# A sliding-window copy: one megabyte moves to the software ring, in parts that are uneven over the DMA engines

## The chip, the cores and the metric

The kernel runs on one core of one Trainium2 chip. The metric is the device time of one execution in microseconds (us). Medians are of three to eleven runs. Two kernels are compared only within one call, on one chip. Four chips come up: "the first" (the prediction and its result), and "the second", "the third" and "the fourth". Where a stretch of one trace is set beside that of another chip, the text says so.

## The reference

```python
def reference(x, window_size, stride):          # x: 32 x 4096 x 256 float32, 64, 32
    batch, length, dim = x.shape
    n_windows = (length - window_size) // stride + 1            # 127
    result = np.zeros((batch, n_windows, window_size, dim), dtype=np.float32)
    for i in range(n_windows):
        start = i * stride
        result[:, i] = x[:, start:start + window_size].copy()
    return result
```

No arithmetic: of HBM, the large memory beside the chip's cores, 134 MB are read and 266 MB written. A window is 64 KB, two consecutive blocks of 32 rows (32 KB each), and each inner block is written twice.

## The kernel before

Three queues feed the same 16 DMA engines. The ACT queue loads every third batch into on-chip memory (11 batches) and stores it twice. The Sync queue copies most of the other batches from HBM to HBM directly, sixteen windows at a time. The software ring, issued by GpSimd, copies what doesn't fit the sixteens ("edges" of fifteen windows, then the last few windows), once the Sync queue is almost done.

```python
    def windows(self, q, b, w0, n, half=None, piece=DIRECT):      # DIRECT = 32768 bytes
        blk = self.blk
        row = [1, 2 * blk if half is None else blk]
        h = half or 0
        return q.dma_start(
            out=self.oap((b * self.nw + w0) * 2 + h, [[2 * blk, n], row]),
            in_=self.xap(b * self.nb + w0 + h, [[blk, n], row]),
            max_dma_last_dim=piece,
        )
# ... columns(): the same with rows cut in 16 parts of 4 KB; load() and store(): the ACT queue's ...

    first_loads, loads, stores = 6 * 17, 5 * 17, 6 * 34
    turns = share = 0
    with tc.tile_critical():
        st.run(ring_s)                                            # all of the ACT queue's work
        for i, (b, w) in enumerate(sixteens):
            sem = near if i == len(sixteens) - 2 else done
            second = turns - first_loads - stores
            loading = turns < first_loads or 0 <= second < loads
            share += 120 if turns < 16 or -8 <= second < 16 else 90 if loading else 18
            if share >= 120:
                share -= 120
                turns += 4
                count(c.windows(ring_d, b, w, 16, 0), done)       # two copies of half rows
                count(c.windows(ring_d, b, w, 16, 1), sem)
            else:
                turns += 3
                count(c.windows(ring_d, b, w, 16), sem)           # one copy of whole rows
            # ... one window by itself, half way ...
        ring_r.wait_ge(near, 16)
        for b, w, n in edges:
            # ... waits for stores of the neighbouring batches ...
            count(c.windows(ring_r, b, w, n), rest)
        count(c.columns(ring_r, last, 116, 9), rest)
        # ... Sync's last two windows, then waits for everything ...
```

`turns` counts packets: an engine serves its queues by turns, one packet each. A whole-row copy gives an engine two packets of 32 KB and a semaphore packet (three turns for 64 KB), a split one two of each (four turns). The share of split ones therefore sets how much the ACT queue moves meanwhile, and so whether all queues end together.

Of the kernel before, what the change touches and what calls it, by code (L numbers as in the profile page):

```python
# [11 lines left out]
class Copier:  # L12
# [27 lines left out]
    def columns(self, q, b, w0, n):  # L40

        part = self.blk // 8
        row = [1, part]
        return q.dma_start(  # L44
            out=self.oap((b * self.nw + w0) * 2, [[part, 16], [2 * self.blk, n], row]),
            in_=self.xap(b * self.nb + w0, [[part, 16], [self.blk, n], row]),
        )

    def load(self, q, t, b, c, rows):
# [76 lines left out]
@with_exitstack  # L126
def kernel(
    ctx: ExitStack,
    tc: tile.TileContext,
    x: bass.AP,  # L130
    window_size: bass.AP,
    stride: bass.AP,
    out: bass.AP,
):
    nc = tc.nc
    W, S = int(window_size), int(stride)
    B, L, D = x.shape
    n_win = (L - W) // S + 1
    assert out.shape == (B, n_win, W, D)
    c = Copier(x, out, B, L, D, W, S, n_win)  # L140


    staged = [*range(1, B, 3)]
    items = [(b, -1 if b == B - 1 else 0, c.nb) for b in staged]
    place = {b: g for g, (b, _, n) in enumerate(items) if n == c.nb}
    direct = [b for b in range(B) if b not in staged]
    pool = ctx.enter_context(tc.tile_pool(name="xb", bufs=1))
    st = Staging(c, tc, pool, x.dtype, items, 6)
    ring_d, ring_s, ring_r = nc.sync, nc.scalar, nc.gpsimd
    done = tc.alloc_semaphore("done")  # L150
    near = tc.alloc_semaphore("near")
    rest = tc.alloc_semaphore("rest")
    total = {done: 0, near: 0, rest: 0}

    def count(dma, sem):
        dma.then_inc(sem, 16)
        total[sem] += 16



    sixteens = []
    for b in direct:
        w = 15 if b - 1 in staged else 0
        sixteens += [(b, w + 16 * j) for j in range((c.nw - w) // 16)]
    singles = [(B - 1, c.nw - 1, 1)]
    edges = [(b, 0 if b - 1 in staged else 112, 15) for b in direct[:-1]]
    last = B - 2
    edges.append((last, 112, 4))

    first_loads, loads, stores = 6 * 17, 5 * 17, 6 * 34  # L170
    turns = share = 0
    with tc.tile_critical():  # L172
        st.run(ring_s)

        for i, (b, w) in enumerate(sixteens):
            sem = near if i == len(sixteens) - 2 else done
            second = turns - first_loads - stores
            loading = turns < first_loads or 0 <= second < loads
            share += 120 if turns < 16 or -8 <= second < 16 else 90 if loading else 18
            if share >= 120:  # L180
                share -= 120
                turns += 4
                count(c.windows(ring_d, b, w, 16, 0), done)
# [3 lines that stand above are left out]
                count(c.windows(ring_d, b, w, 16), sem)  # L187
            if i == len(sixteens) // 2:
                for b, w, half in singles:
                    count(c.windows(ring_d, b, w, 1, half, 2048), done)  # L190

        ring_r.wait_ge(near, 16)
        for b, w, n in edges:
            for k in (b - 1, b + 1):
                if k in place and b != last:
                    st.wait_stored(ring_r, place[k])
            count(c.windows(ring_r, b, w, n), rest)


        count(c.columns(ring_r, last, 116, 9), rest)  # L200
        st.wait_stored(ring_d, place[B - 1])
        count(c.columns(ring_d, last, 125, 2), done)
        total[st.ended] = st.count[st.ended]
        for sem, n in total.items():
            ring_d.wait_ge(sem, n)
# [35 lines left out]
```

## Time and profile before

| kernel before, first chip | |
|---|---|
| median (3 runs) | 752.05 us |
| bytes moved by the DMA engines, mean rate | 313.26 MB, 418 GB/s |
| Sync's last 32 KB packet ends | 656.7 us |
| first ring packet | 658.7 us |
| last data packet of ACT; of the ring | 745.1 us; 745.8 us |

The first lines are from the page of the profile of the kernel before. The rows of 40 give, in slices of 18.7 us, the tenths for which the 16 DMA engines were busy and the GB/s moved. Then come the number of packets, and for each queue its packets, megabytes and share of the engines' time (q1 is Sync, q10 ACT, q0 the ring).

```profile
DMA  8999999999999999999999999999999999999996
GB/s 360 401 427 429 427 429 428 434 423 418 420 424 423 418 424 415 422 427 427 414 427 417 429 432 429 430 422 430 429 423 421 423 421 419 425 426 423 431 409 262
DMA packets 18290, 313.26 MB, mean 418 GB/s; under 512 B 4336, under 2 KB 4336, under 8 KB 4528
...
q1 hardware_dynamic: 8016, 154.32, 48.8%
q10 hardware_dynamic: 9104, 138.41, 44.0%
q0 software_dynamic: 1168, 20.51, 6.5%
...
HBM read 220.95 MB, written 267.09 MB: 651 GB/s over the span
```

The engines are at least nine tenths busy in every slice between the first and the last, so only three things can be gained: a faster start, a faster rate, a shorter end. In the trace's packet records an undisturbed packet of 32 KB takes 1.213 us and one of 16 KB 0.611 us, which is 27 GB/s for an engine and some 432 GB/s for sixteen.

The same view restricted to two stretches: the 15 us from the ring's first packet, and twelve microseconds shortly before the end.

```profile
DMA packets 351, 6.54 MB, mean 436 GB/s; under 512 B 73, under 2 KB 73, under 8 KB 73
...
q0 software_dynamic: 181, 3.97, 62.6%
q10 hardware_dynamic: 170, 2.57, 40.6%
```

Last, the ring's groups of instructions (line, engine, operation, count, then busy us and mean ns, then the idle time before them and what ended it): 22 copies, the first issued when Sync signalled at 654 us.

```profile
L34 POOL DMA_DIRECT2D out_dram<-in_x_dram x21 | 12.0, 576 | 691.3 <-DMA out_dram<-in_x_dram 654.0
L44 POOL DMA_DIRECT2D out_dram<-in_x_dram x1 | 0.6, 581 | 0.0
```

### The profile page before, as it was taken

What the parts mean: (1) busy time and instruction counts of PE and PEld (TensorE: products, weight loads), DVE (VectorE), ACT (ScalarE), POOL (GpSimd) and SP (SyncE); (2) the same over time, 40 slices, a digit from 0 to 9 for tenths busy, and PEclk for the clock granted to TensorE, in tenths of its full rate; (3) what the DMA queues carried; (4) which work ended last, traced back from release to release, by engine and by line L of the source; (5) the groups of instructions that cost most, each with busy time, mean ns of one, the idle gap of its engine ahead of it and who ended that gap; (6) DMA issues with size and microseconds to landing.
All of it is one profiled execution on the core that took longest, in us unless ns stands there. A gap on an engine that the chain in (4) does not pass through costs nothing.

```text
span 749.4 us, 322 instructions
## 1 busy us (share of the span) xinstructions
POOL 12.8 (2%) x26
## 2 busy tenths in 40 slices
POOL 0000000000000000000000000000000000040100
DMA  8999999999999999999999999999999999999996
GB/s 360 401 427 429 427 429 428 434 423 418 420 424 423 418 424 415 422 427 427 414 427 417 429 432 429 430 422 430 429 423 421 423 421 419 425 426 423 431 409 262
DMA packets 18290, 313.26 MB, mean 418 GB/s; under 512 B 4336, under 2 KB 4336, under 8 KB 4528
## 3 DMA queue, kind: packets, MB, share of 16 engines
q1 hardware_dynamic: 8016, 154.32, 48.8%
q10 hardware_dynamic: 9104, 138.41, 44.0%
q0 software_dynamic: 1168, 20.51, 6.5%
q14 instruction: 2, 0.02, 0.0%
HBM read 220.95 MB, written 267.09 MB: 651 GB/s over the span
## 4 chain that ended last, share of the span: by engine, by line
another core or an unknown queue 92%; POOL 2%; issue 0%; POOLq 0%; SPq 0%
POOL out_dram L34 2%; POOL out_dram L44 0%; POOLq L236 0%; SPq L172 0%; POOLq L114 0%
## 5 line engine op out<-in xcount | busy, mean ns | idle before, releaser
L34 POOL DMA_DIRECT2D out_dram<-in_x_dram x21 | 12.0, 576 | 691.3 <-DMA out_dram<-in_x_dram 654.0
L44 POOL DMA_DIRECT2D out_dram<-in_x_dram x1 | 0.6, 581 | 0.0
L222 POOL MEMSET const-float32-0.0<- 128x1 f32 x1 | 0.1, 98 | 0.2 <-issue 0.2
L222 POOL MEMSET const-bfloat16-1.0<- 128x1 bf16 x1 | 0.1, 101 | 0.0
L222 POOL MEMSET const-float32-1.0<- 128x1 f32 x1 | 0.1, 98 | 0.0
L222 POOL MEMSET const-uint8-127<- 128x1 uint8 x1 | 0.1, 98 | 0.0
## 6 DMA issues: line engine op xcount, KB each, us to landing
out_dram<-in_x_dram SPq DMA_DIRECT2D x92, 1024.0 KB, 100.7
out_dram<-xb ACTq DMA_DIRECT2D x21, 4096.0 KB, 139.7
out_dram<-in_x_dram SPq DMA_DIRECT2D x110, 512.0 KB, 90.3
xb<-in_x_dram ACTq DMA_DIRECT2D x10, 4096.0 KB, 131.4
out_dram<-in_x_dram POOLq DMA_DIRECT2D x20, 960.0 KB, 38.5
xb<-in_x_dram ACTq DMA_DIRECT2D x4, 1024.0 KB, 15.7
out_dram<-xb ACTq DMA_DIRECT2D x2, 1024.0 KB, 113.4
out_dram<-xb ACTq DMA_DIRECT2D x4, 512.0 KB, 96.9
```

The source lines that it names most:

```text
L34: return q.dma_start(out=self.oap((b * self.nw + w0) * 2 + h, [[2 * blk, n], row]), in_=self.xap(b * self.nb + w0 + h, [[blk, n], row]), m ...
L44: return q.dma_start(out=self.oap((b * self.nw + w0) * 2, [[part, 16], [2 * self.blk, n], row]), in_=self.xap(b * self.nb + w0, [[part, 16 ...
L222: nc = _bacc.Bacc("TRN2", target_bir_lowering=False, num_devices=1)
```

## The change

The last sixteen windows of the Sync queue (1 MB) go to the ring. In a cycle of the head every engine makes one 32 KB copy and two 16 KB loads. The intent is to set groups of four engines apart by a quarter of that cycle: at the outset three copies of four rows each give 48, 32 and 16 KB to an engine of three groups; the fourth group gets nothing. The remainder follows when Sync is almost done, so that each engine has carried 64 KB. The three constants of the split pattern are retuned for it.

```diff
+    def quarters(self, q, b, w0, p0, n):
+        part = self.blk // 4
+        at = p0 * 2 * part
+        dims = [[part, 2 * n], [1, part]]
+        return q.dma_start(
+            out=bass.AP(self.out.tensor, self.oap((b * self.nw + w0) * 2, dims).offset + at, [[2 * self.blk, 4], *dims]),
+            in_=bass.AP(self.x.tensor, self.xap(b * self.nb + w0, dims).offset + at, [[self.blk, 4], *dims]),
+            max_dma_last_dim=4 * part,
+        )
@@
+    apart = sixteens.pop()
@@
     with tc.tile_critical():
+        for k in range(3):
+            count(c.quarters(ring_r, apart[0], apart[1] + 4 * k, 0, 3 - k), rest)
         st.run(ring_s)
@@
-            share += 120 if turns < 16 or -8 <= second < 16 else 90 if loading else 18
+            share += 120 if turns < 28 or -8 <= second < 16 else 86 if loading else 11
@@
         ring_r.wait_ge(near, 16)
+        for k, p in ((3, 0), (0, 3), (1, 2), (2, 1)):
+            count(c.quarters(ring_r, apart[0], apart[1] + 4 * k, p, 4 - p), rest)
```

`max_dma_last_dim` is in bytes, so 4 * part is 8 KB: the parts go as packets of 8 KB, 6, 4 and 2 to an engine at the outset, 8, 2, 4 and 6 at the end.

## The prediction

> **What bounds it now.** The kernel only moves bytes: the page's DMA part shows 313.26 MB at a mean of 418 GB/s over 749.4 us, the 16 DMA engines busy 9 tenths or more in slices 2 to 39; the chain of waits is 92% DMA. In the trace's packet records an undisturbed 32 KB packet takes 1.213 us, a 16 KB one 0.611, so 16 engines reach about 432 GB/s; 313.26 MB at that rate is 725 us. The missing 24 us:
> - first packet at 2.4 us;
> - a slow head: 239, 393, 405 GB/s up to 8 us, 430 up to 16, then 368 to 404 up to 32 us (16 KB load packets take up to 2.0 us), then 432;
> - 410 to 425 GB/s in most store stretches (32 KB packets at 1.24 to 1.26 us), some 12 us in sum;
> - a drain: engines finish between 740.8 and 745.8 us, the span ends 3.6 us later.
>
> Up to 16 us all engines are in step: a 32 KB direct copy, then two 16 KB loads, a cycle of 2.43 us. From 50 us on phases are scattered.
>
> **What the change does.** 1 MB leaves the Sync queue for the software ring. At the outset three copies with four outer rows give 48, 32, 16 and 0 KB to four groups of engines; the remainder (16, 32, 48, 64 KB) follows when the Sync queue is almost done. The Trainium skill, "DMA: Bandwidth & Descriptors", section "Why a DMA increments its semaphore by 16 and not by 1", says that a software-ring copy with k below 16 runs on k consecutive engines from a round-robin cursor; four rows then mean four engines. No view of before shows it. 16 KB is 0.61 us, a quarter cycle: the groups should run a quarter cycle apart, so copies (HBM read and write) and loads (read only) mix evenly at once, not after 34 us. Split pairs on the Sync queue fall from 55 to 48, with the moved block 10 turns per engine fewer; Sync ends some us before its present 656.7 us and leaves ACT about 2.5 MB more for the last stretch. The ring's small packets give turns back to ACT, so I expect ring and ACT still to end together.
>
> **Costs.** No byte added. 8 packets of 8 KB instead of 2 of 32 KB per engine, at some 10 ns fixed each (2 x 0.611 - 1.213), and seven semaphore packets of 9 ns: 0.1 us. Ring packets came 4.3 us after issue at 654 us; at the outset I expect them at 3 to 5 us. The issues (0.58 us each) are on an idle engine.
>
> **On the critical path.** Only the head and, by chance, the drain. Lost against 432 GB/s: 17 us at about 390 (1.6 us), 0.6 us at 4 to 8 us, 0.4 us at 43 to 48: 2.6 us. I expect over half back, 1.5 to 2 us. The store stretches have scattered phases already: nothing changes there. The drain may move by 1 to 2 us either way.
>
> **Prediction: 750.2 us, range 747.6 to 752.6; faster by over 2%: 0.01, within 2%: 0.98, slower by over 2%: 0.01.**
>
> **Right shows as:** 0.38 MB of 8 KB ring packets before 8 us on 12 engines; slices 1 and 2 above 365 and 415 GB/s; 16 to 32 us above 415; middle slices as before; drain again 5 us wide. **Wrong:** the dip persists though groups are staggered (then addresses, not phases); ring packets come too late; ring or ACT ends well ahead; the lag of 48 KB widens the drain.
>
> **What would make it wrong.** Uneven engine speeds decide the drain; the copies may not land on distinct groups; slow store stretches may depend on the queues' shares, which the new split pattern moves.

## More of the kernel before

```profile
DMA packets 375, 4.94 MB, mean 411 GB/s; under 512 B 135, under 2 KB 135, under 8 KB 172
...
q0 software_dynamic: 165, 2.94, 59.8%
q10 hardware_dynamic: 162, 1.87, 38.2%
q1 hardware_dynamic: 48, 0.13, 2.8%
```

The view counts a packet where it starts, so a short stretch can show a little more than 432 GB/s. As soon as the ring starts, it takes 3.97 MB of 6.54 and ACT 2.57; near the end both still run side by side. That mix matters: the ring's copies read and write HBM, ACT's stores only write it.

## The result, and the profile after

The changed kernel is slower: 756.08 us (755.71 to 756.55, 6 runs) against 751.9 us, ratio 1.0055, 95% interval 1.0041 to 1.0068. A ratio is the mean time of one kernel's fast runs over that of the other's of the same rounds, so it is not quite the ratio of the quoted medians. The time lies above the range predicted.

The same lines of the page of the changed kernel:

```profile
DMA  8999999999999999999999999999999999999996
GB/s 360 419 428 429 425 425 429 429 419 421 418 422 417 425 412 425 421 425 423 409 424 412 433 419 423 431 430 428 423 418 425 412 424 416 426 415 433 412 398 220
DMA packets 18754, 313.26 MB, mean 415 GB/s; under 512 B 4704, under 2 KB 4704, under 8 KB 4896
...
q1 hardware_dynamic: 7856, 153.27, 48.3%
q10 hardware_dynamic: 9104, 138.41, 43.8%
q0 software_dynamic: 1792, 21.56, 7.2%
...
HBM read 220.95 MB, written 267.09 MB: 647 GB/s over the span
```

The bytes are the same. The ring has 624 packets more, and only 128 of them are the megabyte in packets of 8 KB. The other 496 are packets of 4 bytes. The packet records show what they are. While a four-row copy runs, each of the four engines that carry it has a packet of 8 KB where each of the twelve others has one of 4 bytes; then all sixteen have one more, the semaphore's. That makes 12 x 32 + 16 x 7 = 496, without remainder. The kernel before follows the same rule: its 20 edges of two packets leave one engine idle, the copy of four windows leaves twelve, the one in columns none, and 20 x (2 + 16) + (12 x 2 + 16) + 16 = 416.

So the seven copies occupy 32 + 7 turns on every engine, data or not: 15 at the outset, 24 at the end. The kept records do not name the engine of a packet; what runs on which is read from these counts and from the times. The 15 us from the ring's first packet at the end show the price:

```profile
DMA packets 748, 6.43 MB, mean 429 GB/s; under 512 B 320, under 2 KB 320, under 8 KB 320
...
q10 hardware_dynamic: 374, 5.65, 88.9%
q0 software_dynamic: 374, 0.78, 13.4%
```

Ring and ACT have 374 packets each, one for one. But by the packet records the ring's are 291 of 4 bytes, 79 of 8 KB and 4 of 32 KB, and ACT's are 345 of 16 KB and 29 of 4 bytes (the semaphores'), so ACT moves 5.65 MB and the ring 0.78, where before the ring moved 3.97. Sync ended at 651.6 us, the ring's first packet came at 653.4 us, its first large copy at 667.8 us. By then ACT had 11.7 MB left; before, it had 14.7 MB at the same point. ACT then runs out first, as ten microseconds near the end show:

```profile
DMA packets 207, 3.51 MB, mean 351 GB/s; under 512 B 82, under 2 KB 82, under 8 KB 90
...
q0 software_dynamic: 165, 3.15, 89.5%
q10 hardware_dynamic: 42, 0.36, 10.1%
```

The engines are as busy as ever, yet move 351 GB/s. The ring's 32 KB packets take some 1.48 us here instead of 1.21. The ring's bytes are both read from and written to HBM, ACT's only written; with each packet shared out over its duration, these ten microseconds carry 671 GB/s of HBM traffic. The Trainium skill, "HBM Reference", section "Specifications (TRN2)", gives about 716 GB/s for a domain, and this stretch lies somewhat below that. So a limit of HBM fits, but it is argued and not shown: the first stretch of the kernel before carried as much, 670 GB/s by the same count, while half of the ring's 32 KB packets took the undisturbed 1.213 us. What is shown is that the rate falls when the ring is left alone; with ACT's stores beside it, 12 us near the end ran at 411 GB/s before.

The ring's groups of instructions after the change:

```profile
L54 POOL DMA_DIRECT2D out_dram<-in_x_dram x7 | 4.3, 624 | 646.7 <-DMA out_dram<-in_x_dram 645.6
L34 POOL DMA_DIRECT2D out_dram<-in_x_dram x21 | 11.9, 571 | 29.9 <-DMA out_dram<-xb 29.9
L44 POOL DMA_DIRECT2D out_dram<-in_x_dram x1 | 0.6, 573 | 0.0
```

There are 29 copies instead of 22. The trace's records of the last instructions, which these views leave out, show a second price. After all data has landed, a drain on GpSimd takes 2.437 us, where it took 1.865 us before. From the last data packet to the end of the span it is 4.6 us, 3.6 us before.

### The profile page after: what moved, and what is told of

Read it like the earlier page. It is cut to its first block, busy times and chain, and to the rows that moved or that the text cites. A ratio compares the mean times of both kernels' runs of the same rounds, so it can differ in the third digit from the quotient of the medians.

```text
span 754.8 us, 320 instructions
## 1 busy us (share of the span) xinstructions
POOL 17.0 (2%) x33
## 4 chain that ended last, share of the span: by engine, by line
another core or an unknown queue 89%; POOL 2%; issue 0%; PEldq 0%
POOL out_dram L34 2%; POOL out_dram L54 1%; POOL out_dram L44 0%; PEldq L254 0%
## 5 line engine op out<-in xcount | busy, mean ns | idle before, releaser
L54 POOL DMA_DIRECT2D out_dram<-in_x_dram x7 | 4.3, 624 | 646.7 <-DMA out_dram<-in_x_dram 645.6
L34 POOL DMA_DIRECT2D out_dram<-in_x_dram x21 | 11.9, 571 | 29.9 <-DMA out_dram<-xb 29.9
L44 POOL DMA_DIRECT2D out_dram<-in_x_dram x1 | 0.6, 573 | 0.0
```

What stands on the lines that cost most here:

```text
L34: return q.dma_start(out=self.oap((b * self.nw + w0) * 2 + h, [[2 * blk, n], row]), in_=self.xap(b * self.nb + w0 + h, [[blk, n], row]), m ...
L44: return q.dma_start(out=self.oap((b * self.nw + w0) * 2, [[part, 16], [2 * self.blk, n], row]), in_=self.xap(b * self.nb + w0, [[part, 16 ...
L54: return q.dma_start(out=bass.AP(self.out.tensor, self.oap((b * self.nw + w0) * 2, dims).offset + at, [[2 * self.blk, 4], *dims]), in_=bas ...
```

## The experiments

Theory A: the ring's empty turns hold its large copies back at the end, ACT drains alone, then the ring copies alone at some 350 GB/s. Rival B: the new split pattern costs. Rival C: the lag itself, or the moved megabyte, widens the drain of the engines. Theory D, for the last microsecond: the closing drain grows with the number of ring copies. Expectations in microseconds were written for the first chip (before: 751.9 us) and are read as ratios.

| run | chip | median, us | before, us | ratio | 95% interval |
|---|---|---|---|---|---|
| changed kernel | first | 756.08 | 751.9 | 1.0055 | 1.0041 to 1.0068 |
| split pattern alone (e1_shares_only) | second | 746.68 | 745.51 | 1.0010 | 0.9998 to 1.0022 |
| parts, old split pattern (e2_parts_old_shares) | second | 751.01 | 745.51 | 1.0075 | 1.0063 to 1.0088 |
| parts as whole rows (e3_whole_rows) | second | 748.70 | 745.51 | 1.0040 | 1.0028 to 1.0052 |
| remainder after the edges (e4_rest_late) | second | 747.39 | 745.51 | 1.0024 | 1.0013 to 1.0036 |
| before, again (b0_before_again) | third | 745.48 | 745.45 | 1.0000 | 0.9989 to 1.0012 |
| changed, again (a0_after_again) | third | 749.06 | 745.45 | 1.0050 | 1.0038 to 1.0063 |
| before, nine ring copies for one (e5_nine_columns) | third | 746.62 | 745.45 | 1.0013 | 1.0001 to 1.0025 |
| parts on all 16 engines (e6_even_parts) | third | 746.36 | 745.45 | 1.0010 | 0.9996 to 1.0024 |
| two packets to a row (e7_two_packets) | fourth | 746.13 | 745.01 | 1.0020 | 1.0006 to 1.0034 |
| remainder in 4 KB packets (e9_half_packets_late) | fourth | 754.07 | 745.01 | 1.0119 | 1.0106 to 1.0133 |

### The split pattern alone

```diff
 kernel before
-            share += 120 if turns < 16 or -8 <= second < 16 else 90 if loading else 18
+            share += 120 if turns < 28 or -8 <= second < 16 else 86 if loading else 11
```

> The kernel before with the three new constants of the split pattern alone (28, 86, 11), no parts. Theory A (the four-row copies put a 4-byte packet on the 12 idle engines for each of their packets, so the remainder at the end holds the ring's large copies back for 24 turns, ACT drains alone, and the ring then copies alone at some 350 GB/s): about 751.5 us, within 750 to 753, since ACT then outlasts the ring a little and costs nothing. Rival B (the new split pattern costs: slower middle, other balance): 754 to 756 us, and bytes moved by 650 us about 0.8 MB behind before.

The ratio is 1.0010, within theory A's range (751.5 of 751.9 is 0.9995, 753 is 1.0015) and below rival B's. Bytes moved by 640 us are 272.13 MB; the kernel before, on the third chip, where it takes as long, moved 272.28. B falls: the pattern is not what costs.

### The parts with the old split pattern

```diff
 changed kernel
-            share += 120 if turns < 28 or -8 <= second < 16 else 86 if loading else 11
+            share += 120 if turns < 16 or -8 <= second < 16 else 90 if loading else 18
```

> The changed kernel with the old constants (16, 90, 18). Theory A: still held back by 24 turns, and ACT has about 1.6 MB less left when the Sync queue ends (16.3 instead of 17.9 MB), so the ring is alone for longer: 756 to 758 us, slower than the changed kernel. Rival B: 750 to 752 us.

The ratio is 1.0075, worse than the changed kernel, as theory A said. At the first large ring copy ACT has 10.1 MB left; ACT ends at 731.3 us, the ring at 744.1. The retuned constants were right in direction: they leave ACT more for the end. They do not make up for 24 turns.

### The parts as whole rows

```diff
 changed kernel
-        dims = [[part, 2 * n], [1, part]]
+        dims = [[1, 2 * n * part]]
-            max_dma_last_dim=4 * part,
+            max_dma_last_dim=DIRECT,
```

> The changed kernel with the same bytes as whole rows of 16 to 32 KB, so 10 turns of packets instead of 32 (6 instead of 20 at the end). Theory A: the 4-byte packets of the software ring fall from 912 to 648 (12 x 10 + 7 x 16 + 416), the first 32 KB ring packet of the large copies comes about 6 us after the ring's first packet at the end instead of 15, ring and ACT end together, 749.5 to 751.5 us. Rival B: 754 to 756 us still.

This run missed. The 4-byte packets are 648, as counted, and ACT and ring end within a microsecond of each other (740.3 and 741.3 us). But the ratio is 1.0040, in rival B's range. One microsecond is the longer end, found here first (4.6 us after the last packet). Another difference is seen in the packets of the head. By their times, a copy of 32 KB rows and one of 16 KB rows, one packet to an engine, landed on the same four engines as the first copy, so these four were given 96 KB and the others nothing; the ring did not move on. The edit changed two things, then, and does not test theory A cleanly. The last edit but one below does.

### The remainder after the edges

```diff
 changed kernel
-        for k, p in ((3, 0), (0, 3), (1, 2), (2, 1)):
-            count(c.quarters(ring_r, apart[0], apart[1] + 4 * k, p, 4 - p), rest)
         for b, w, n in edges:
             ...
+        for k, p in ((3, 0), (0, 3), (1, 2), (2, 1)):
+            count(c.quarters(ring_r, apart[0], apart[1] + 4 * k, p, 4 - p), rest)
         count(c.columns(ring_r, last, 116, 9), rest)
```

> The changed kernel with the remainder issued after the ring's large copies instead of before them, its form unchanged. Theory A: the large copies start some 2 us after the Sync queue ends, ACT and ring run together to the end, 750 to 752 us although every packet and filler is there. Rival B, and rival C (the lag of 48 KB itself or the moved megabyte widens the drain): 754 us or more.

All packets and all empty turns are still there (912 of 4 bytes), only later. The ring's large copies start at 646.5 us, 1.4 us after Sync ends; ACT and ring end at 738.4 and 740.2 us. The ratio falls to 1.0024, half of the changed kernel's. That is under the range of B and C (754 is 1.0028, which the interval still includes), and above that of A (752 is 1.0001), which did not know of the longer end: 4.5 us after the last packet here too.

### Both kernels once more, on one chip

No edit.

> The kernel before, unchanged, for its profile and noise beside the others of this call. All theories: ratio 1.000 within 0.002; ring's last clean-up on GpSimd about 1.87 us. If the head's dip of the first profile (12.6 MB by 34 us, 19.4 MB by 50 us) is a steady trait of this kernel, it is there again; if it was chance, up to 0.7 MB more by 50 us.

> The changed kernel, unchanged, beside the others. Theory A: ratio about 1.005 to 1.006 on this chip as well, first large ring copy about 15 us after the ring's first packet at the end, ACT done some 5 us or more before the ring, and 340 to 360 GB/s in the stretch that the ring copies alone; bytes moved by 650 us within 0.3 MB of before's (the 0.8 MB deficit of the first pair of profiles was chance).

The ratios are 1.000 and 1.005. The two spans are 743.6 and 747.7 us, and the packet records divide the 4.1 us between them:

- Up to 640 us the changed kernel moved 272.05 MB, the one before 272.28: 0.5 us. The profiles of the second and third chip lie between 271.9 and 272.4 MB (without the one that fell on its kernel's slowest run), so this is not told from chance.
- From 640 us to the last packet, 41.0 MB took 100.0 us before and 41.2 MB took 103.2 us after: 2.6 us beyond the 0.5.
- From the last packet to the end: 3.6 us before, 4.6 us after: 1.0 us.

The middle term has two parts, found by asking when each kernel had moved the same number of bytes. From 285 to 305 MB the two go at the same pace. The last 8 MB cost 1.5 us, and these are theory A's: the first large ring copy comes at 661.8 us, 14.8 us after the ring's first packet; ACT ends at 736.4 us, the ring at 743.2; from 728 to 740 us the rate is some 355 GB/s.

The other 1.0 us is lost between 280 and 285 MB, just where the ring's large copies begin and ACT still has plenty. Theory A has no place for it. The packet records of all runs give the rate in the ten microseconds from the first large ring copy on:

| before that copy, the ring had | GB/s in the ten microseconds |
|---|---|
| nothing at the end: kernel before (first, third chip), e1, e5, e4 | 429, 428, 431, 431, 430 |
| the remainder on all 16 engines: e6 | 422 |
| the remainder on groups of four: changed kernel (first, third chip), e2, e3, e7, e9 | 397, 390, 403, 393, 400, 379 |

For e3 and e7, whose remainder has 32 KB packets too, the start of the large copies is counted off from the number of those. So the uneven remainder has a second price, 0.6 to 1.2 us if 430 GB/s is taken as the undisturbed rate (an estimate from this table). It is a comparison of traces that were made for other questions; why the rate dips was not tested.

In the first chip's pair of profiles the changed kernel was also 0.8 MB, 1.9 us, behind by 640 us. The third chip's pair, 0.2 MB apart, does not repeat it.

The head answers the prediction's main point. From 16 to 34 us the first profile, that of the kernel before on the first chip, had its dip (the changed kernel there: 416 GB/s):

```profile
DMA packets 461, 7.24 MB, mean 402 GB/s; under 512 B 142, under 2 KB 142, under 8 KB 142
```

The same view of the kernel before and then of the changed one, both on the third chip, has:

```profile
DMA packets 481, 7.62 MB, mean 423 GB/s; under 512 B 144, under 2 KB 144, under 8 KB 144
```

```profile
DMA packets 598, 7.59 MB, mean 421 GB/s; under 512 B 246, under 2 KB 246, under 8 KB 246
```

On this chip there is no dip to cure: 423 GB/s without the lag, 421 with it. By 50 us the kernels had moved 19.98 and 19.89 MB. In the first chip's profiles it was 19.42 before and 19.83 MB after, so a gain of 1.0 us may have been real there; it is one profile of each, and on the third chip it is absent.

### More ring copies, nothing else

```diff
 kernel before
-        count(c.columns(ring_r, last, 116, 9), rest)
+        for k in range(9):
+            count(c.columns(ring_r, last, 116 + k, 1), rest)
```

> The kernel before with its ring copy of nine windows in columns issued as nine copies: same bytes and packets, eight more copies on the ring (30 instead of 22). Theory D (the last drain on GpSimd costs some 0.08 us for each copy that the ring ever took, after all data has landed): drain 2.5 us instead of 1.87 us, time up by 0.6 us (ratio 1.0009, at the edge of what shows). Rival (the drain waits for the length of the last copies' data or for the parts' form): drain stays at 1.87 us.

The drain takes 2.514 us with 30 copies. With 1.865 us for 22 and 2.437 us for 29, that is 0.08 us for each copy that the ring took (0.65 us for eight more). Theory D holds. The time rose by a ratio of 1.0013, a microsecond, with an interval that starts at 1.0001. The drain explains 0.65 us of it; here Sync's last wait also ended 0.4 us later after the last packet than in the kernel before.

### Parts on all sixteen engines

```diff
 changed kernel: sixteen rows in each copy, 8 KB wide (the last 16 KB), 3 copies at the outset and 4 at the end (cut: `at` and the two calls, changed to fit)
-        dims = [[part, 2 * n], [1, part]]
+        dims = [[1, n * part]]
-            out=... [[2 * self.blk, 4], *dims]), in_=... [[self.blk, 4], *dims]), max_dma_last_dim=4 * part
+            out=... [[2 * self.blk, 16], *dims]), in_=... [[self.blk, 16], *dims]), max_dma_last_dim=DIRECT
```

> The changed kernel with the same megabyte on the ring in as many copies and at the same points, but each copy with 16 rows, so that all engines carry equal parts and none lags: 384 KB at the outset, 640 KB at the end. If the lag between groups of engines is worth something at the head (the intent of the change), this is slower by 1 us or more than the whole rows with a lag (ratio 1.004), and moves at least 0.2 MB less by 50 us; if the lag is worth nothing, it is equal to that or faster, 1.002 to 1.004, with a drain of 2.44 us on GpSimd as in all kernels with 29 ring copies.

The ratio is 1.0010, the lowest of all kernels that put the megabyte on the ring (the intervals of this one and the next overlap). There is no lag, and no idle engine, so no empty turns but the semaphores'. It was faster than expected even for a lag that is worth nothing. Its profile fell on its slowest run (748.42 us; 1.35 MB behind the kernel before by 640 us), so its stretches are not compared. The lag is not missed.

### Two packets to a row

```diff
 changed kernel
-            max_dma_last_dim=4 * part,
+            max_dma_last_dim=4 * n * part,
```

> The changed kernel with only the packet size of the seven part copies raised, so that each row goes as two packets of 8 to 32 KB (the same bytes on the same four engines, if the ring rotates as it did with 8 KB packets): 14 packet turns instead of 32, 8 + 4 instead of 20 + 4 at the end. Theory A: 4-byte packets of the ring 416 + 12 x 14 + 7 x 16 = 696; large ring copies start some 8 us after the ring's first packet at the end, not 15; ACT and ring end within 2 us of each other; ratio 1.002 to 1.003, of which 1.0 us is the longer end (clean-up of 29 ring copies, a fetch). If the lag of groups of engines itself, not the turns, costs: ratio stays at 1.004 to 1.005.

One argument of the changed kernel is another: the same bytes on groups of four engines (three different groups at the outset, by the times of the packets), in 14 packet turns instead of 32. All numbers came as theory A had them: 696 packets of 4 bytes, the large copies 7.4 us after the ring's first packet (some 8 were expected), ACT and ring ending at 738.4 and 739.5 us, ratio 1.0020. The 15 us from the ring's first packet at the end:

```profile
DMA packets 516, 6.29 MB, mean 419 GB/s; under 512 B 192, under 2 KB 192, under 8 KB 192
...
q10 hardware_dynamic: 253, 3.93, 62.2%
q0 software_dynamic: 263, 2.36, 40.1%
```

The ring moves 2.36 MB in them, three times as much as with 8 KB packets. Here the lag is whole, and by 50 us the kernel has moved 19.99 MB, against 19.98 in the kernel before on the third chip. Of its remaining 0.2% over the kernel before, the longer end (4.6 us after the last packet) is some 1.0 us; the dip at the start of the large copies is there too (400 GB/s in the table above).

### The remainder in packets of 4 KB

```diff
 changed kernel, the four copies at the end only
-            max_dma_last_dim=4 * part,
+            max_dma_last_dim=4 * part // 2,
```

> The changed kernel with the packets of the remainder alone halved to 4 KB: 40 + 4 turns at the end instead of 20 + 4, same bytes, same number of copies. Theory A: 4-byte packets of the ring 912 + 12 x 20 = 1152; large ring copies start about 27 us (44 x 0.61) after the ring's first packet at the end; ACT has some 6 to 7 MB left then, ends by about 720 us, and the ring copies alone for over 20 us at 350 to 360 GB/s; ratio 1.008 to 1.012. If turns of the ring don't matter: 1.005 as the changed kernel.

The suspected cost is doubled and the time follows: ratio 1.0119. There are 1152 packets of 4 bytes; the first large ring copy comes 26.4 us after the ring's first packet (44 turns); ACT has 6.4 MB left then. The 15 us from the ring's first packet, and twenty microseconds after ACT has ended (718.6 us):

```profile
DMA packets 789, 6.41 MB, mean 427 GB/s; under 512 B 326, under 2 KB 326, under 8 KB 422
...
q10 hardware_dynamic: 394, 6.01, 93.7%
q0 software_dynamic: 395, 0.39, 7.5%
```

```profile
DMA packets 363, 6.43 MB, mean 321 GB/s; under 512 B 145, under 2 KB 145, under 8 KB 170
...
q0 software_dynamic: 363, 6.43, 96.7%
```

In the first stretch the ring has as many turns as ACT and a fifteenth of its bytes. In the second it is alone, at 321 GB/s, less than the 350 to 360 expected.

No experiment made a kernel that beats the one before. The runs point to fewer ring copies, worth 0.08 us each; joining edges in pairs would have halved them, but such a copy has four dimensions at 32 KB packets and does not build ("Unable to balance aps with more than 3 dims"), so it was not tried on the chip.

## Why the prediction was wrong

- **"The ring's small packets give turns back to ACT, so I expect ring and ACT still to end together."** This step failed. It counted 8 packets of 8 KB and 7 semaphores on an engine, because it assumed that a four-row copy leaves twelve engines alone. It takes a turn on every engine for each of its packets: 39 turns in all, 24 of them at the end. For 14 to 15 us, where the ring's large copies should have run, ACT moved nine tenths of the bytes; it then ended some 7 us before the ring (743.3 and 750.2 us on the first chip, 736.4 and 743.2 us on the third). That is 1.5 of the 2.6 us lost from 640 us to the last packet on the third chip. It is shown from both sides: moved out of the way (1.0024), thinned (1.0020), doubled (1.0119). The prediction also had no dip at the start of the large copies; it is the other 1.0 us, and its cause stays open.
- **"Costs: 0.1 us."** Mis-sized. The packets themselves are that cheap; seven more ring copies lengthen the closing drain on GpSimd by 0.57 us, and the end by 1.0 us in all. The other 0.4 us lie mostly between the end of that drain and the start of the Sync engine's own closing drain (0.4 us in the changed kernel, 0.1 us in the one before, and 0.1 us again in the run with the parts and the old pattern, which ends 4.0 us after its last packet). Their cause was not settled.
- **"I expect over half back, 1.5 to 2 us" at the head.** Not found. Where both kernels ran on one chip, the rate from 16 to 34 us was 423 GB/s before and 421 after, and the bytes by 50 us were equal to 0.1 MB, and hardly more were moved with the lag in its cleanest form (fourth chip). The dip on which the sum was built was in one profile of the first chip; it was taken for a trait of the kernel. Nor did the lag come as early as foretold. The ring's first packet came at 5.9 us, not at 3 to 5; by the times of the packets the second group's parts began at about 13.4 us and the third's at 19.2 us, because each copy must first pass its turns on all engines.
- **What held.** The mechanism of four rows on four engines; no byte added; Sync ends earlier (651.6 us for 656.7) and leaves ACT 2.3 MB more (17.9 MB for 15.6 at that moment; 2.5 were foretold); the drain of the engines is again 5 us wide. The chance given to "within 2%" was right, but the sign inside it was not.

What stays open, beside the dip, is why whole rows (1.0040) are slower than two packets to a row (1.0020). The copies that fell on the same four engines are the difference that was seen, but it was not tried by itself.

## What to carry to other kernels

Count a queue's work in turns, not only in bytes. Engines that serve their queues packet by packet give a queue of small or empty packets as many turns as a queue of large ones, and whoever is behind it in the same ring waits. A copy on the software ring that uses few engines should have few, large packets; better still, let it use all sixteen, since here the copies that followed uneven ones also began at a lower rate. When a span is longer, ask at which byte the time was lost: one plausible cause can hide a second. And a dip seen in one profile is not yet a trait to be tuned for: take a second profile, on another chip if there is one, before a change is built on it.

## What the Trainium skill lacked or had wrong

- "DMA: Bandwidth & Descriptors", section "Why a DMA increments its semaphore by 16 and not by 1", says that a software-ring copy with k below 16 runs on k consecutive engines, while all 16 post the semaphore. The counts of packets agree (the kept records don't say which engines), but the page lacks that the other 16 - k engines also get a 4-byte packet for each packet of the copy: 912, 648, 696 and 1152 packets of 4 bytes in four kernels, each equal to the count by that rule.
- The same section has the engines chosen by a round-robin cursor. By the times of the packets (no record names the engine), copies of four rows with two or more packets to an engine moved on to another group; at the outset of one run, two copies with one packet to an engine, 32 KB and then 16 KB, landed on the four engines of the copy before them, which so carried 96 KB each.
- The same page, section "Queues, rings and completion order", says that an engine serves its queues in turn, packet by packet. The trace agrees (374 packets each of ring and ACT in 15 us). It lacks the consequence that 4-byte packets take whole turns: 0.78 MB against 5.65 MB.
- The same page, "Specifications", gives about 1 us to the first byte on the GpSimd path. From the start of the issue to the ring's first packet it was 4.3 us at the outset (1.56 to 5.9 us) and at the end (649.08 to 653.4 us; before the change 654.39 to 658.7 us).
- No page has that the closing drain on GpSimd grows with the ring's copies: 1.865 us for 22, 2.437 us for 29, 2.514 us for 30.
